# A layer norm and the products around it, made in two halves of the tokens

## The chip, the cores and the metric

The kernel runs on one core of a Trainium2 chip. The metric is the device time of one launch in microseconds. A core has a matrix engine (PE, with its weight loads PEld), a vector engine (DVE), a scalar engine (ACT), a general engine (POOL) and a queue that mostly issues DMAs (SP). Each works through its own list of instructions in order and waits for the others by semaphores.

## The reference, cut to what matters

Two streams of tokens go through a trunk of two layers: x (512 tokens of 1024 features) and ctx (256 tokens), which share all weights. Each layer has three sub-layers, and each ends in a layer norm over the features of a token:

```
def post_norm(x, h, g, b):
    return layer_norm(DEEPNORM_ALPHA * x + h, g, b)
def modulate(h, m, i):
    return h * (1.0 + m[:, :, 3 * i + 1]) + m[:, :, 3 * i]
def swiglu(u, wg, wu, wd):
    return (jax.nn.silu(u @ wg) * (u @ wu)) @ wd
def half_ffn(h, m, i, wg, wu, wd, g, b):
    u = modulate(h, m, i)
    return post_norm(h, 0.5 * m[:, :, 3 * i + 2] * swiglu(u, wg, wu, wd), g, b)
...
h_x = half_ffn(h_x, m_x, 0, ...)                                   # 1024 -> 2816 -> 1024
mix_x, mix_c = token_mixing(modulate(h_x, m_x, 1), modulate(h_c, m_c, 1), ...)
h_x = post_norm(h_x, m_x[:, :, 5] * (mix_x @ w_out[l]), ...)
h_x = half_ffn(h_x, m_x, 2, ...)
```

`token_mixing` is one input projection followed by gated linear attention, windowed attention and an RWKV recurrence. The ctx stream needs no output of its last mixing, so only x runs to the end. So x passes six layer norms, and each lies between a product that makes its input (the FFN's second product with `wd`, or `w_out`) and a product that needs its output (the FFN's first products with `wg` and `wu`, or the input projection); the sixth makes the output.

## The kernel before, in words

Everything is kept feature-major: a tile is 128 features by all tokens of the stream, and a stream (`X`, 512 columns, or `C`, 256) has KT = 8 such tiles. Every product is made in a split float32: weights and data are cut into hi + lo, and each k-tile takes three matmuls, hi x hi, hi x lo and lo x hi (`product`, line 348 the matmul). A weight block of up to four k-tiles is loaded by `load_split`: a DMA, an ACT copy that rounds to hi (line 323), and a subtraction for lo (line 326), alternately on DVE and POOL. Two matmul operands can be seen in a row's name: `pyx<-hhx,l_dx` is the bank `py` of x, from the hidden tile's hi part and the lo part of the weight block `d`.

An FFN makes 22 hidden tiles (`hidden(m)`: banks `pg` and `pu`, then `sg`, `hh`, `hl`), in six groups of four or three. After each group it makes eight tiles `py` of the second product and adds each to the residual `r[j]` on DVE (line 437). In the last group `ln_stat` runs beside it: the sum of r over the feature tiles in `acc1` (POOL, line 470) and that of the squares in `acc2` (ACT squares, line 467; DVE adds, line 472). `wout` does the same with the eight tiles `po` of the output projection.

Then `ln_next` makes the norm. `ln_apply` sums over partitions on PE (banks `lnst`, `lnsq`, line 488), makes mean and 1 / deviation of the 512 tokens (`lnms`: DVE, ACT and a DVE reciprocal, line 505), spreads both over all partitions on PE (`lnm`, `lnb`, line 493) and subtracts the mean from the eight r tiles (line 515: three on DVE, five on POOL). Then for each tile: `ut` on DVE (line 538), its hi part `uh` on ACT (line 543), its lo part `ul` on DVE (line 544; for two tiles of eight on POOL, line 354). The next product starts with `uh0`. The residual of the next sub-layer, alpha * h, is made after the last `ul`: eight instructions on DVE (line 548) and eight on ACT. At the end `ln_out` writes the output (line 558 on DVE, then ACT, then a DMA) in place of u.

The order of the work is fixed when the program is built: the code is written as a sequence, and a scheduler of the build lays out each engine's list from it by its own estimates of what will be ready first. Two streams' stages written one after the other may thus run beside each other: the first stages of x run beside the mixing of ctx, and from about 2020 us on x is alone (its second layer's mixing runs from about 2690 to 3075 us, its last part to the end).

The six norms of x stand in the trace of before at about 881 us (after the first FFN; its next product is the input projection), 1848 (after `wout` of layer 0), 2273 (between the two FFNs), 2654 (before the second input projection), 3123 (after `wout` of layer 1) and 3502 us (the end). They are called the first to the sixth norm below. The ctx stream's first norm, at 285 us, runs with 256 columns.

## Time and profile before

| | us |
|---|---|
| time, median of 3 runs | 3524.95 (3523.06 to 3531.83) |
| span of the profiled execution, first to last instruction | 3523.2 |
| PE busy | 3295.0 (94%) |
| DVE, POOL, ACT busy | 1824.8 (52%), 1513.6 (43%), 1489.5 (42%) |
| x alone, before the third norm (2100 to 2200): PE busy | 100% |
| around the third norm (2200 to 2300): PE busy, granted clock | 87.3%, 0.90 |
| around the fourth (2600 to 2700) | 81.1%, 0.88 |
| around the fifth (3100 to 3200) | 90.7%, 0.93 |

The profiled execution's span is its own time within what the three runs scatter; nothing of size lies around it. [...] PE is full between the norms and has a gap at each of them, and a table by stretches of time shows how long each engine worked in a gap.

### The profile page before, as it was taken

The page shows a single profiled execution, that of the slowest core. Times are in us where ns is not written, and L with a number is a line of the kernel's source. Part 1 is how long each engine was busy: PE and PEld are TensorE (multiplying, and loading weights), DVE is VectorE, ACT ScalarE, POOL GpSimd, SP SyncE. Part 2 cuts the span into 40 slices and gives each one's busy share as a digit, 9 for nine tenths or more (in the row PEclk, how much of TensorE's full clock was granted, in tenths as well). Part 3 has the DMA queues.
Part 4 walks back from the last instruction along what each step waited for, and adds up shares of the span by engine and source line. Part 5 has one row for each costly group of instructions (what it writes and reads, how often), then busy time and mean ns, then how long its engine had stood idle before and what let it go on. Part 6 is the DMA issues. An engine that isn't in the chain of part 4 may idle for free. (4 is left out here: it accounts for less than half of the span.)

```text
span 3523.2 us, 63899 instructions
## 1 busy us (share of the span) xinstructions
PE 3295.0 (94%) x24774; PEld 2668.2 (76%) x24774; DVE 1824.8 (52%) x3198; ACT 1489.5 (42%) x2835; POOL 1513.6 (43%) x1375
## 2 busy tenths in 40 slices
PE   7999999999899999999989999899997997889997
PEld 4797667776677788789867888688885765678886
DVE  2545453445865556566767332542237666762224
ACT  2445333444553445456644433343335335643233
POOL 2554432434644455564454333533345343263335
PEclk8999999999999999999999999999998987999999
DMA  8765444344355543334242333223322210033332
GB/s 300 238 193 172 138 123 136 127 128 142 125 160 181 175 123 115 101 101 130 92 126 65 103 100 96 82 88 98 96 87 72 62 49 11 30 102 96 96 96 75
DMA packets 279135, 407.77 MB, mean 116 GB/s; under 512 B 76464, under 2 KB 101040, under 8 KB 278832
## 3 DMA queue, kind: packets, MB, share of 16 engines
q1 hardware_dynamic: 272064, 397.53, 36.2%
q10 hardware_dynamic: 6768, 6.16, 0.6%
q8 instruction: 195, 3.19, 0.4%
q14 instruction: 108, 0.88, 0.1%
HBM read 390.20 MB, written 13.39 MB: 115 GB/s over the span
## 5 line engine op out<-in xcount | busy, mean ns | idle before, releaser
L348 PE MATMUL pyx<-hhx,l_dx 128*128 128x512 f32 x704 | 277.7, 395 | 4.4 <-DVE l_dx L326 3.2
L348 PE MATMUL pyx<-hhx,h_dx 128*128 128x512 f32 x704 | 275.5, 393 | 0.3 <-ACT h_dx L323 0.3
L348 PE MATMUL pyx<-hlx,h_dx 128*128 128x512 f32 x704 | 275.5, 391 | 0.0
L437 DVE SCALAR_TENSOR_TENSOR rx<-pyx,gtx,rx 128x512 f32<-128x512 f32 x192 | 143.0, 748 | 239.2 <-PE pyx L348 239.1
L326 POOL TENSOR_TENSOR l_ux<-r_ux,h_ux 128x512 fp32r<-128x512 f32 x88 | 114.5, 1301 | 316.5 <-ACT h_ux L323 308.8
L323 ACT ACTIVATE h_dx<-r_dx 128x512 fp32r<-128x512 f32 (+1 forms) x192 | 113.5, 595 | 297.3 <-PE pyx L348 117.8
L323 ACT ACTIVATE h_ux<-r_ux 128x512 fp32r<-128x512 f32 x176 | 111.0, 631 | 280.0 <-PE pgx L348 137.7
L348 PE MATMUL pgx<-uhx,h_gx 128*128 128x512 f32 x528 | 209.2, 396 | 16.1 <-ACT uhx L543 16.1
L323 ACT ACTIVATE h_gx<-r_gx 128x512 fp32r<-128x512 f32 x176 | 111.0, 630 | 267.1 <-PE pyx L348 93.7
L348 PE MATMUL pgx<-ulx,h_gx 128*128 128x512 f32 x528 | 207.6, 393 | 5.9 <-DVE ulx L544 5.9
L326 POOL TENSOR_TENSOR l_dx<-r_dx,h_dx 128x512 fp32r<-128x512 f32 (+1 forms) x96 | 117.4, 1225 | 215.0 <-ACT h_dx L323 201.3
L326 POOL TENSOR_TENSOR l_gx<-r_gx,h_gx 128x512 fp32r<-128x512 f32 x88 | 120.0, 1363 | 204.4 <-ACT h_gx L323 196.0
L348 PE MATMUL pgx<-uhx,l_gx 128*128 128x512 f32 x528 | 207.4, 393 | 0.0
L348 PE MATMUL pux<-uhx,h_ux 128*128 128x512 f32 x528 | 207.1, 392 | 0.0
L348 PE MATMUL pux<-uhx,l_ux 128*128 128x512 f32 x528 | 206.5, 391 | 0.0
L348 PE MATMUL pux<-ulx,h_ux 128*128 128x512 f32 x528 | 206.4, 391 | 0.0
L354 POOL TENSOR_TENSOR hlx<-sgx,hhx 128x512 fp32r<-128x512 f32 x88 | 115.2, 1309 | 151.7 <-ACT hhx L353 151.4
L326 DVE TENSOR_TENSOR l_ux<-r_ux,h_ux 128x512 fp32r<-128x512 f32 x88 | 64.4, 731 | 205.9 <-ACT h_ux L323 205.3
L277 PE MATMUL ada<-wa,sc 128*32 128x256 f32 x1152 | 147.5, 405 | 19.7 <-DMA wa<-in_ada 14.2
L348 PE MATMUL pyc<-hhc,h_dc 128*128 128x256 f32 x528 | 154.9, 295 | 7.2 <-DVE rc L437 5.6
L348 PEld LDWEIGHTS pyx<-hhx,l_dx 128*128 128x128 f32 x704 | 132.6, 188 | 37.3 <-DVE l_dx L326 5.2
L348 PEld LDWEIGHTS pyx<-hhx,h_dx 128*128 128x128 f32 x704 | 132.6, 188 | 32.0 <-ACT h_dx L323 3.0
(800 smaller groups left out, 10153.3 us busy)
## 6 DMA issues: line engine op xcount, KB each, us to landing
wa<-in_ada SPq DMA_DIRECT2D x288, 256.0 KB, 3.8
r_gx<-in_wg SPq DMA_DIRECT2D x176, 256.0 KB, 2.7
r_ux<-in_wu SPq DMA_DIRECT2D x176, 256.0 KB, 2.7
r_gc<-in_wg SPq DMA_DIRECT2D x132, 256.0 KB, 3.0
r_uc<-in_wu SPq DMA_DIRECT2D x132, 256.0 KB, 3.0
r_dx<-in_wd SPq DMA_DIRECT2D x128, 256.0 KB, 2.7
r_dc<-in_wd SPq DMA_DIRECT2D x96, 256.0 KB, 3.0
r_ix<-in_win SPq DMA_DIRECT2D x84, 256.0 KB, 2.7
```

Of the source, the lines that this page charges most:

```text
L277: nc.tensor.matmul(ps[32 * g:32 * g + 32, :256], self.sc[:, k, 6 - 2 * cc:38 - 2 * cc], w[:, x, :], start=cc == 0 and k < 4, stop=cc == 3 ...
L323: nc.scalar.activation(hi[:, :n], raw[:, :n], AF.Copy)
L326: e.tensor_tensor(lo[:, :n], raw[:, :n], hi[:, :n].bitcast(F32), ALU.subtract)
L348: nc.tensor.matmul(ps[:, :N], wt[:, k, :], mv[kk][:, :N], start=kk == 0 and a == 0, stop=kk == n - 1 and a == 2)
L354: self.nc.gpsimd.tensor_tensor(lo, src, hi.bitcast(F32), ALU.subtract)
L437: nc.vector.scalar_tensor_tensor(r[j], py[:, :n], gt[:, j:j + 1], r[j], ALU.mult, ALU.add)
```

## The change

The columns of x are cut into two halves of 256 tokens (`Stream.halves`); ctx has one. Four things are then done by halves:

- The last group of an FFN and the output projection are made in two passes over the eight feature tiles (`passes`), the first for half 0, the second for half 1. Each product has 256 columns instead of 512. The second pass begins with those feature tiles whose split weights are still held (`keep`; four tiles of eight in the FFNs of `rest`, two in `wout`, one in the first FFN); the weights of the others are loaded and split again.
- After each pass `after(h)` makes the norm of that half: sums, reciprocal, spread, subtraction, u and alpha * h. The instructions are as many as before for each half, with half the columns.
- The first hidden tile of the FFN behind a norm, and the first tile of the input projection (number 6), are made half by half, with their weights kept between.
- The scratch tiles `uf`, `sq`, `ut` and `lnms` share one pool of six buffers of 256 columns; sums and mean share one PSUM bank.

Besides, the spreading of the statistics takes a broadcast column (`eq`) in place of a loaded matrix (`eg`), the banks `pg` and `pu` of a hidden tile are claimed together, and the mixing's outputs change places (RWKV to tiles 2 and 3, attention to 4 to 7, the rows of `w_out` with them). Comments are removed, so line numbers shift: the matmul stays line 348, the split of weights becomes 319 and 322, the residual 452, the sums 484, 491 and 495, the statistics 512 to 530, the subtraction 540, u 576 to 582, alpha * h 587, the output 603.

```diff
...
+        self.halves = [slice(c, c + 256) for c in range(0, n, 256)]
...
-    def product(self, ps, ap, mh, ml, n, N, name, lane="f"):
         nc = self.nc
         step = self.step(n)
         for k0 in range(0, n, step):
             w = min(step, n - k0)
-            hi, lo = self.pre.pop((name, k0), None) or self.load_split(ap, k0, w, f"{name}_{k0}", lane)
+            key = name, k0
+            wt2 = self.kept.pop(key, None) or self.pre.pop(key, None)
+            hi, lo = wt2 or self.load_split(ap, k0, w, f"{name}_{k0}", lane)
+            if keep:
+                self.kept[key] = hi, lo
             for k in range(w):
                 for a, (wt, mv) in enumerate(((hi, mh), (hi, ml), (lo, mh))):
                     kk = k0 + k
-                    nc.tensor.matmul(ps[:, :N], wt[:, k, :], mv[kk][:, :N],
+                    nc.tensor.matmul(ps[:, cols], wt[:, k, :], mv[kk][:, cols],
                                      start=kk == 0 and a == 0, stop=kk == n - 1 and a == 2)
+    def passes(self, s, units):
+        nk = (self.wpool["f"][2] - 1) // units if len(s.halves) > 1 else 0
+        order = list(range(KT))
+        for h, cols in enumerate(s.halves):
+            for pos, j in enumerate(order):
+                yield h, cols, pos, j, h == 0 and j >= KT - nk
+            order = list(range(KT - nk, KT)) + list(range(KT - nk - 1, -1, -1))
...
-            pg = pmm("pg" + nm)
-            self.product(pg, self.ins["wg"][f, l, m], s.uh, s.ul, KT, n, "g" + nm)
-            pu = pmm("pu" + nm)
-            self.product(pu, self.ins["wu"][f, l, m], s.uh, s.ul, KT, n, "u" + nm)
+            pg, pu = pmm("pg" + nm), pmm("pu" + nm)
+            parts = s.halves if m == 0 and normed else [slice(0, n)]
+            for cols in parts:
+                keep = cols is not parts[-1]
+                self.product(pg, self.ins["wg"][f, l, m], s.uh, s.ul, KT, cols, "g" + nm, keep=keep)
+                self.product(pu, self.ins["wu"][f, l, m], s.uh, s.ul, KT, cols, "u" + nm, keep=keep)
...
-            for j in range(KT):
-                py = pmm(f"py{s.name}{l}{f}_{gi}_{j}")
-                self.product(py, self.ins["wd"][f, l, j, :, k0:k1], hh, hl, k1 - k0, n, f"d{s.name}{l}{f}_{gi}_{j}")
-                nc.vector.scalar_tensor_tensor(r[j], py[:, :n], gt[:, j:j + 1], r[j], ALU.mult, ALU.add)
+            for h, cols, pos, j, keep in (self.passes(s, 1) if k1 == FT else
+                                          ((0, slice(0, n), j, j, False) for j in range(KT))):
+                py = pmm(f"py{s.name}{l}{f}_{gi}_{j}_{h}")
+                self.product(py, self.ins["wd"][f, l, j, :, k0:k1], hh, hl, k1 - k0, cols, f"d{s.name}{l}{f}_{gi}_{j}",
+                             keep=keep)
+                nc.vector.scalar_tensor_tensor(r[j][:, cols], py[:, cols], gt[:, j:j + 1], r[j][:, cols],
+                    self.ln_stat(s, h, pos, j, r, pool)
+                    if pos == KT - 1:
+                        after(h)
...
+        if pos < KT - 2:
+            nc.gpsimd.tensor_tensor(s.acc1[:, cols], s.acc1[:, cols], r[j][:, cols], ALU.add)
+        else:
+            s.last.append(r[j][:, cols])
+        if pos < KT - 1:
...
+        q = 64
+        ps = self.pln("lnst")
+        sv = ps[:, 0:q], ps[:, q:2 * q]
...
+                nc.tensor.matmul(ps[:, g * q:(g + 1) * q], self.c["eq"][:, g:g + 1].to_broadcast([P, P]), t,
+                                 start=True, stop=True)
+        stat(0, s.acc1[:, cols], True, False)
+        stat(0, s.last[0], False, False)
+        stat(0, s.last[1], False, True)
+        stat(1, s.acc2[:, cols], True, False)
...
+        mean, rs = s.shift[:, cols], s.acc2[:, cols]
+        mb = ps[:, 256:512]
         spread(mb, ms[:, 0])
-        nc.scalar.activation(mean, mb[:, :n], AF.Copy)
-        b = self.pln("lnb")
+        nc.scalar.activation(mean, mb, AF.Copy)
+        b = self.pmm("lnb")[:, 0:256]
         spread(b, ms[:, 2])
-        nc.scalar.activation(rs, b[:, :n], AF.Copy)
+        nc.scalar.activation(rs, b, AF.Copy)
         for j in range(KT):
             e = nc.gpsimd if j >= 3 else nc.vector
-            e.tensor_tensor(r[j], r[j], mean, ALU.subtract)
+            e.tensor_tensor(r[j][:, cols], r[j][:, cols], mean, ALU.subtract)
         return rs
...
+        def after(h):
+            cols = s.halves[h]
+            if h == 0:
+                vectors()
+            if h == len(s.halves) - 1:
+                prefetch()
+            A, B, ag = v["A"], v["B"], v["ag"]
+            rs = self.ln_apply(s, h, r, pool)
             for j in range(KT):
-                nc.vector.scalar_tensor_tensor(r[j], r[j], ag[:, 0, j:j + 1], rs, ALU.mult, ALU.mult)
-                nc.scalar.activation(r[j], r[j], AF.Identity, bias=ag[:, 1, j:j + 1])
-                if rdst is not None:
-                    nc.sync.dma_start(rdst[:, j, :], r[j])
+                hi, lo, rj = s.uh[j][:, cols], s.ul[j][:, cols], r[j][:, cols]
+                t = pool.tile([P, 256], F32, name="ut", tag="uf", bufs=UF)
+                nc.vector.scalar_tensor_tensor(t, rj, A[:, j:j + 1], rs, ALU.mult, ALU.mult)
+                if j in (2, 5):
+                    nc.scalar.activation(t, t, AF.Identity, bias=B[:, j:j + 1])
+                    self.split(hi, lo, t)
+                else:
+                    nc.scalar.activation(hi, t, AF.Identity, bias=B[:, j:j + 1])
+                    last = nc.vector.scalar_tensor_tensor(lo, t, B[:, j:j + 1], hi.bitcast(F32), ALU.add, ALU.subtract)
+            with self.tc.issue_after(last.ins):
+                for j in range(KT):
+                    rj = r[j][:, cols]
+                    nc.vector.scalar_tensor_tensor(rj, rj, ag[:, 0, j:j + 1], rs, ALU.mult, ALU.mult)
+                    nc.scalar.activation(rj, rj, AF.Identity, bias=ag[:, 1, j:j + 1])
+                    if rdst is not None:
+                        nc.sync.dma_start(rdst[:, j, cols], rj)
...
+        for h, cols, pos, j, keep in self.passes(s, 2):
+            py = self.pmm(f"po{s.name}{l}_{j}_{h}")
+            self.product(py, self.ins["wout"][l, j], s.mh, s.ml, KT, cols, f"o{s.name}{l}_{j}", keep=keep)
+            nc.vector.scalar_tensor_tensor(r[j][:, cols], py[:, cols], gt[:, j:j + 1], r[j][:, cols], ALU.mult, ALU.add)
+            self.ln_stat(s, h, pos, j, r, pool)
+            if pos == KT - 1:
+                after(h)
...
```

The order of the instructions on two engines around the third norm follows. Names are tile, head or layer and group numbers: `pyx01_5_7` is the FFN product of x in layer 0, FFN 1, group 5 (the last), feature tile 7, and after the change a last `_0` or `_1` tells the half. On PE before, from the last product of the pass to the first product behind the norm:

```order
L348 MATMUL pyx01_5_7_25292<-hhx01_21_25140,l_dx01_5_7_0_25296 128x512
L488 MATMUL lnst_25360<-acc1_25161,c_ones_m_132 32x128 [waits Pool_49]
L488 MATMUL lnst_25360<-rx1_6_22061,c_ones_m_132 32x128 [waits DVE_49]
L488 MATMUL lnsq_25361<-acc2_25162,c_ones_m_132 32x128 [waits DVE_49]
L488 MATMUL lnst_25360<-rx1_7_22062,c_ones_m_132 32x128 [waits DVE_49]
L488 MATMUL lnsq_25361<-sq_25309,c_ones_m_132 32x128 [waits Activation_49]
L493 MATMUL lnm_25388<-lnms_25382,c_eg_22053 128x128 [waits DVE_49]
L493 MATMUL lnb_25394<-lnms_25382,c_eg_22053 128x128 [waits DVE_49]
L348 MATMUL pgx10_0_25458<-uhx0_1_0_25320,h_gx10_0_0_25338 128x512 [waits Activation_49]
```

And on PE after, from the last product of half 0 to the first of half 1:

```order
L348 MATMUL pyx01_5_7_0_26051<-hhx01_21_25899,l_dx01_5_7_0_26055 128x256
L512 MATMUL lnst_26095<-acc1_25920,c_ones_m_132 32x64 [waits PE_49,Pool_49]
L512 MATMUL lnst_26095<-rx1_6_22365,c_ones_m_132 32x64 [waits DVE_49]
L512 MATMUL lnst_26095<-rx1_7_22366,c_ones_m_132 32x64 [waits DVE_49]
L512 MATMUL lnst_26095<-acc2_25921,c_ones_m_132 32x64 [waits DVE_49]
L512 MATMUL lnst_26095<-sq_26068,c_ones_m_132 32x64 [waits Activation_49]
L517 MATMUL lnst_26095<-lnms_26116,c_eq_142 128x64 [waits DVE_49]
L517 MATMUL lnb_26127<-lnms_26116,c_eq_142 128x64 [waits DVE_49]
L348 MATMUL pyx01_5_4_1_26191<-hhx01_19_25582,h_dx01_5_4_0_25990 128x256
```

What moved: half of the pass's products now stand behind the statistics of half 0, and the same block of statistics comes a second time behind them (not shown). PE goes through its list in order, so the products of half 1 are not issued until the statistics of half 0 have been made. On DVE before, behind the reciprocal of the same norm:

```order
L505 RECIPROCAL lnms_25382<-lnms_25382 128x128 [waits Activation_49]
...
L544 SCALAR_TENSOR_TENSOR ulx6_1_0_25334<-ut_25434,Bx1_0_25312,uhx6_1_0_25326 128x512 [waits Activation_49]
L544 SCALAR_TENSOR_TENSOR ulx7_1_0_25335<-ut_25438,Bx1_0_25312,uhx7_1_0_25327 128x512 [waits Activation_49]
L548 SCALAR_TENSOR_TENSOR rx1_0_22055<-rx1_0_22055,agx1_0_25317,acc2_25162 128x512
...
L548 SCALAR_TENSOR_TENSOR rx1_7_22062<-rx1_7_22062,agx1_0_25317,acc2_25162 128x512
L326 TENSOR_TENSOR l_ux10_1_0_25557<-r_ux10_1_0_25554,h_ux10_1_0_25556 128x512 [waits DMAHW6_49,PE_49,Activation_49]
```

And on DVE after, behind the reciprocal of half 0, with the work of both halves in one list:

```order
L530 RECIPROCAL lnms_26116<-lnms_26116 128x64 [waits Activation_49]
...
L582 SCALAR_TENSOR_TENSOR ulx1_1_0_26088<-ut_26145,Bx1_0_26071,uhx1_1_0_26080 128x256 [waits Activation_49]
L452 SCALAR_TENSOR_TENSOR rx1_4_22363<-pyx01_5_4_1_26191,gtx0_2_23714,rx1_4_22363 128x256 [waits PE_49]
L322 TENSOR_TENSOR l_dx01_5_2_0_26274<-r_dx01_5_2_0_26271,h_dx01_5_2_0_26273 128x384 [waits DMAHW1_49,Activation_49]
...
L582 SCALAR_TENSOR_TENSOR ulx7_1_0_26094<-ut_26171,Bx1_0_26071,uhx7_1_0_26086 128x256 [waits Activation_49]
L587 SCALAR_TENSOR_TENSOR rx1_0_22359<-rx1_0_22359,agx1_0_26076,acc2_25921 128x256
...
L587 SCALAR_TENSOR_TENSOR rx1_7_22366<-rx1_7_22366,agx1_0_26076,acc2_25921 128x256
L495 TENSOR_TENSOR acc2_25921<-acc2_25921,sq_26215 128x256 [waits Activation_49]
L452 SCALAR_TENSOR_TENSOR rx1_3_22362<-pyx01_5_3_1_26249,gtx0_2_23714,rx1_3_22362 128x256 [waits PE_49]
L322 TENSOR_TENSOR l_gx10_0_4_26339<-r_gx10_0_4_26336,h_gx10_0_4_26338 128x512 [waits DMAHW5_49,Activation_49]
...
L526 COPY lnms_26375<-lnst_26354 128x64 [waits PE_49]
L530 RECIPROCAL lnms_26375<-lnms_26375 128x64 [waits Activation_49]
```

What moved: u of half 0 and the residuals, squares and weight splits of half 1 (lines 452, 495, 322) share DVE's list, and alpha * h of half 0 (line 587) now stands ahead of most of half 1's sums and thus ahead of the second reciprocal.

## Rows read from the trace of the kernel before

**Rows 1.** Stretches: length, each engine's busy us (instructions), granted clock, DMA share, GB/s.

```profile
2100.00:2200.00 100.00, 100.00 (x443) 82.81 (x442) 29.29 (x44) 29.38 (x48) 30.39 (x24) 1.00 0.31 96
2200.00:2300.00 100.00, 87.31 (x395) 69.47 (x394) 56.81 (x71) 37.38 (x65) 54.77 (x39) 0.90 0.24 74
```

**Rows 2.** Stretches at the third norm: pass, statistics, making u, rest of hidden tile.

```profile
2253.60:2270.20 16.60, 16.60 (x72) 13.17 (x71) 12.23 (x14) 8.00 (x14) 11.40 (x8) 1.00 0.31 96
2270.20:2282.60 12.40, 6.83 (x58) 4.25 (x56) 10.40 (x15) 5.50 (x11) 5.68 (x5) 0.72 0.23 78
2282.60:2298.60 16.00, 8.89 (x23) 6.55 (x24) 15.87 (x17) 6.64 (x10) 9.58 (x6) 0.57 0.00 0
2298.60:2303.70 5.10, 5.10 (x24) 4.22 (x23) 5.10 (x8) 3.75 (x6) 1.78 (x1) 1.00 0.00 0
```

**Rows 3.** DVE's timeline, third norm: start, us, instruction, idle before and its releaser.

```profile
2259.03 1.41 DVE L437 SCALAR_TENSOR_TENSOR rx<-pyx,gtx,rx 128x512 f32<-128x512 f32 x2 [4.05 <-PE pyx L348]
```

**Rows 4.** Waits, third norm: who waited for whom, us in total, times, longest.

```profile
PE pgx L348 <- ACT uhx L543: 5.8, 1, 5.8
```

**Rows 5.** DVE's groups by form, 2100 to 2310: count, busy us, mean ns, idle before.

```profile
L437 DVE SCALAR_TENSOR_TENSOR rx<-pyx,gtx,rx 128x512 f32<-128x512 f32 x31 | 23.1, 748 | 37.9 <-PE pyx L348 37.9
L538 DVE SCALAR_TENSOR_TENSOR ut<-rx,Ax,acc 128x512 f32<-128x512 f32 x8 | 8.6, 1119 | 0.0
L472 DVE TENSOR_TENSOR acc<-acc,sq 128x512 f32<-128x512 f32 x6 | 8.6, 1426 | 0.2
L548 DVE SCALAR_TENSOR_TENSOR rx<-rx,agx,acc 128x512 f32<-128x512 f32 x8 | 6.4, 870 | 0.0
L544 DVE SCALAR_TENSOR_TENSOR ulx<-ut,Bx,uhx 128x512 fp32r<-128x512 f32 x6 | 6.0, 1046 | 0.1
L326 DVE TENSOR_TENSOR l_dx<-r_dx,h_dx 128x384 fp32r<-128x384 f32 x8 | 4.5, 558 | 9.3 <-ACT h_dx L323 9.3
L515 DVE TENSOR_TENSOR rx<-rx,shift 128x512 f32<-128x512 f32 x3 | 4.0, 1397 | 0.8 <-ACT shift L509 0.8
```

**Rows 6.** DVE's groups by form, 160 to 305, ctx's 256 columns.

```profile
L437 DVE SCALAR_TENSOR_TENSOR rc<-pyc,gtc,rc 128x256 f32<-128x256 f32 x32 | 15.2, 480 | 16.9 <-PE pyc L348 16.8
L538 DVE SCALAR_TENSOR_TENSOR ut<-rc,Ac,acc 128x256 f32<-128x256 f32 x8 | 5.5, 740 | 0.6 <-ACT acc L512 0.6
L472 DVE TENSOR_TENSOR acc<-acc,sq 128x256 f32<-128x256 f32 x6 | 4.1, 692 | 1.3 <-ACT sqt L476 1.2
L544 DVE SCALAR_TENSOR_TENSOR ulc<-ut,Bc,uhc 128x256 fp32r<-128x256 f32 x6 | 3.4, 603 | 0.1
L548 DVE SCALAR_TENSOR_TENSOR rc<-rc,agc,acc 128x256 f32<-128x256 f32 x6 | 2.5, 476 | 0.0
L515 DVE TENSOR_TENSOR rc<-rc,shift 128x256 f32<-128x256 f32 x3 | 2.3, 801 | 0.0
```

**Rows 7.** Stretches at ctx's first norm: pass, statistics, making u.

```profile
273.90:285.30 11.40, 9.89 (x74) 8.93 (x72) 9.26 (x16) 6.32 (x14) 8.28 (x9) 1.00 0.01 2
285.30:290.20 4.90, 3.44 (x54) 2.33 (x53) 2.71 (x8) 3.23 (x9) 0.56 (x1) 1.00 0.61 191
290.20:302.80 12.60, 12.60 (x73) 9.68 (x72) 11.50 (x20) 6.50 (x16) 8.33 (x9) 1.00 0.66 218
```

**Rows 8.** A stretch of PE within ctx's FFN, all matmuls with 256 columns.

```profile
210.00:220.00 10.00, 10.00 (x86) 1.00 0.67 197
```

**Rows 9.** Stretches at the fifth norm: pass, rest of the hidden tile.

```profile
3076.90:3123.00 46.10, 46.10 (x195) 37.62 (x196) 24.06 (x23) 15.86 (x28) 33.61 (x23) 0.94 0.48 154
3145.20:3150.20 5.00, 5.00 (x24) 4.14 (x23) 5.00 (x8) 4.32 (x8) 1.67 (x1) 1.00 0.00 0
```

**Rows 10.** Stretches at the sixth norm: pass, statistics, output.

```profile
3483.00:3499.50 16.50, 16.50 (x73) 13.33 (x71) 9.72 (x14) 5.58 (x11) 8.71 (x7) 1.00 0.05 12
3499.50:3506.60 7.10, 3.96 (x49) 2.98 (x48) 5.50 (x8) 4.24 (x8) 2.64 (x2) 0.76 0.00 0
3506.60:3519.30 12.70, 1.16 (x8) 0.97 (x8) 12.36 (x11) 5.63 (x10) 8.45 (x5) 0.73 0.25 95
```

More of the change, by code (lines that the diff above doesn't have):

```diff
@@ L29 @@
 GMAX = 5
+UF = 6
 NMOD = 9
@@ L212, in setup @@
         self.nsplit = 0
-        self.nada, self.tail, self.pre = 8, None, {}
+        self.nada, self.tail, self.pre, self.kept = 8, None, {}, {}
         self.wnames = []
```

181 lines of the change are left out of this document (79 added, 102 removed).

## The prediction

> **What bounds the kernel now.** I read the table of stretches first. Where x is alone and no norm is near, PE is busy for all of 100 us and does 443 matmuls of 512 columns, 226 ns each, while DVE works 29 us [rows 1]. The stretch with the third norm has the same work in it and PE is busy 87.3 us; DVE's share doubles [rows 1]. So the time is PE's, except at the six norms, and there I asked which engine PE waits for.
>
> The table of the third norm, cut at its steps, answers that [rows 2]. The reader should see three things. In the pass (2253.6 to 2270.2) PE does 72 matmuls without a gap. While u is made (2282.6 to 2298.6) DVE is busy 15.87 of 16.0 us and PE gets 23 matmuls done, at a granted clock of 0.57. The waits name the releaser as ACT's `uh`, 5.8 us for the first one [rows 4], but ACT is busy 6.64 of the 16.0 us [rows 2] and only rounds what DVE has made. So the gap is as long as DVE's list: from the first product to the last u it takes 45.0 us, of which DVE is busy 12.23 + 10.40 + 15.87 = 38.5 and idle 6.5, most of that the 4.05 us ahead of the first residual [rows 2, 3]. The first hidden tile ends 5.1 us later, at +50.1 us from the pass's first product.
>
> **The change part by part.** *Matmuls.* 864 matmuls of 512 columns become twice as many of 256. In ctx's FFN 86 of these take 10.0 us [rows 8], 116 ns each, so a pair costs 232 instead of 226: some 5 us in all if every one were on the path. At the FFN norms they are not, since DVE sets the time there; at `w_out` they are in the sums below.
>
> *DVE's list at an FFN norm.* Per norm it has eight residuals, six additions of squares, three subtractions, eight `ut`, six `ul`, eight alpha * h. With 512 columns that is 8 x 0.748 + 8.6 + 4.0 + 8.6 + 6.0 + 6.4 = 39.6 us [rows 5]. How long they take with 256 columns beside x's POOL work, no trace shows; ctx's first norm has the same instructions with 256 columns: 8 x 0.480 + 4.1 + 2.3 + 5.5 + 3.4 + 8 x 0.476 = 23.0 us [rows 6], 0.58 of it, so two halves take 45.9. What counts is what lies before the last u. Before: 39.6 less alpha * h, 33.2. After: 45.9 less alpha * h of half 1 alone (3.8), and the four reloaded weight blocks, two of them split on DVE at 0.558 [rows 5]: 43.2. So DVE has 10.0 us more to do. The other end is that a half costs exactly a half: 39.6 - 3.2 + 1.1 = 37.5, 4.3 us more, of which alpha * h of half 0, now ahead of half 1's sums, is three quarters.
>
> *Idle time of DVE there.* PE's list has the statistics of half 0 ahead of all products of half 1, so nothing of half 1 fills them. The first residual comes earlier, since its product has half the columns (about -2.0 us of the 4.05). The statistics now stop DVE twice; ctx's took 4.9 us with DVE busy 2.71 [rows 7], so +2.2. Idle: 6.5 - 2.0 + 2.2 = 6.7.
>
> *What is gained.* Products of half 1 run beside u of half 0, and hidden half 0 beside u of half 1. Behind the last u only the second product of hidden half 1 is left, 24 x 0.116 = 2.8 us instead of 5.1.
>
> *Third norm.* Last u at 38.5 + 10.0 + 6.7 = 55.2 (49.5 with exact halves), hidden tile done at 58.0 (52.3) against 50.1: +2.2 to +7.9. I take **+6**, nearer to ctx's rows, which are the same instructions beside the same subtractions on POOL, but a little less, since x's first modulation ran beside them.
>
> [...]
>
> *Fourth norm* (towards the input projection). The same list; but before, the next weights were split behind 6.4 us of alpha * h, and now behind 3.8, so the range falls by 2.5: 0 to +5.5, taken **+4**.
>
> *Sixth norm* (the output). DVE is busy 9.72 + 5.50 + 12.36 = 27.6 of 36.3 us and idle 8.7 [rows 10]. Its list is residual, squares, subtraction and output, the last taken as `ut`: 27.2 us with 512 columns, 2 x 15.7 = 31.5 in halves, and 1.1 of reloads: +5.4; idle as above +0.2. The other end: exact halves (+1.1), and idle time down to 4.5, because the sums on POOL, which DVE waits for there, also halve. Range -3 to +6, taken **+4**.
>
> *Fifth norm* (`w_out`, then the FFN). Here PE is busy throughout the pass, 46.1 us, and DVE only 24.06 of it [rows 9], so room exists. Before, from first product to the end of the hidden tile: 73.3 us (3076.9 to 3150.2). After: half 0's pass 192 x 0.116 = 22.3; statistics, during which PE is idle, 4.9 [rows 7]; the pass of half 1, 22.3 by PE, but DVE then owes u (11.2), alpha * h (3.8), residuals and squares (7.9) and about eight splits (twelve reloaded blocks and four of the FFN, half of them on DVE, at 0.558 x 4/3): 28.8; statistics 4.9; u 9.3 to 11.2; tail 2.8. That is 66.5 to 74.9, so -6.8 to +1.6; taken **-2**. The *second norm* is the same beside ctx's recurrence, where DVE has more to do: -5 to +5, taken **0**. The *first* (first FFN, then the input projection): one feature tile's weights are kept instead of four, so seven are split again; and ctx's `w_out` products, which filled x's gap, stand behind the second statistics in PE's list now. The trace has no pair to price this; between the fourth norm's gain undone and its worst: -2 to +9, taken **+3**.
>
> The loaded matrix that goes, the banks claimed together and the exchanged outputs I cost at nothing: the DMA ends long before its use, and the output products wait for all eight mixing tiles at either order but for a few matmuls.
>
> **Sum.** 6 + 4 + 4 - 2 + 0 + 3 = +15 us on the profiled 3523.2, 3538; the median of the runs is 1.75 above that span, so **3540 us**. Lows add up to -15, highs to +35.
>
> **Rivals.**
> 1. *The gap closes*: PE set free at +16.3 (11.4 + 4.9, rows 7) does half 1's products in 8.4, then statistics 4.9, u at exact half cost 9.3, tail 2.8: +41.7 instead of 50.1, -8.4. With the fourth alike, the fifth and second at -6.8, the first at -5 and the sixth at 0: -36, **3489**. [...] For it speaks the second half of the gap, in which PE does a third of its pace. Against it: DVE would have to do u and alpha * h of half 0 and residuals and squares of half 1, 22 us or more, in the 8.4 us of PE's pass, and it was saturated already (15.87 of 16.0, rows 2).
> 2. *It cancels*: `w_out` norms at their low ends pay for the FFN norms: within 10 us, **3525**. For it: halves that cost a half put the sum near -5. Against: alpha * h of half 0 is in the window at any price.
> [...]
> 4. That the halves don't overlap at all: in PE's list half 1's products stand behind the statistics of half 0, but ahead of anything that needs u, so this is excluded.
>
> **How the numbers follow.** What a measurement of this kernel can tell from no change is about 0.3%, 10.6 us. My forecast (norms longer, above 3535.5) 0.39, rival 3 0.12: slower 0.51. Rival 2: 0.22. Rival 1 and the stretch between it and no change, with the low ends of all terms: 0.27. The forecast's own range is 3528 to 3556; to hold 8 in 10 it must take in rival 2, most of rival 3 and the upper part of rival 1's side: 3503 to 3568.
>
> **What would show it.** At the third norm of the changed kernel: DVE busy almost without a gap from the first residual to the last u, last u at about 55 us from the pass's first product; PE idle through the statistics of half 0 and waiting on residuals (its banks) in the second pass; 256-column instructions at 0.58 of the 512-column ones. At the fifth: a second pass of some 25 us. I am wrong if the second pass runs at PE's pace (8.4 us) with the sums of half 1 done right behind it, if DVE's instructions take half or less, or if the `w_out` norms give more than 7 us each.

## The result, and the profile after

The changed kernel takes 3620.49 us (median; 3610.66 to 3628.0) against 3524.73: 1.027 of it, 95% interval 1.0249 to 1.0288. It is slower, as forecast, but by 95.8 us where 15 were forecast, far above the range. Its profiled execution spans 3618.6 us; PE's busy time grows from 3295.0 to 3357.2 us, DVE's from 1824.8 to 1880.7, and the mean granted clock (TensorE's, as a share of full speed) falls from 0.959 to 0.947.

Where the time went is read by cutting both traces at the first residual addition on DVE of the last group of each FFN, and of the first group of the next. A residual of 256 columns comes about 2 us earlier than one of 512 (the first at the third norm 3.5 us behind the start of its pass, before 5.4), so an FFN is taken together with the norm behind it; while ctx runs beside x, ctx's residuals make the cuts. In us, of one profiled execution each; behind the column of before, differences from it (e3, e4, e12 and e15 are experiments, below):

| stretch | before | forecast | after | e3: no halves | e15: u in halves | e4: norm in halves | e12: whole `w_out`, alpha * h last |
|---|---|---|---|---|---|---|---|
| start, to x's first residual | 403.6 | none | +12.8 | -3.4 | -3.8 | +12.5 | +13.6 |
| x's first FFN and first norm | 644.7 | +3 | +9.7 | -4.4 | -1.0 | +10.0 | +12.5 |
| ctx's FFNs, first mixing, second norm | 891.2 | 0 | +21.4 | -7.1 | -1.8 | +22.3 | -4.1 |
| FFN and third norm | 411.3 | +6 | +8.4 | -0.4 | -0.7 | +4.7 | +15.0 |
| FFN, fourth norm, second mixing | 738.6 | +4 | +8.4 | +2.6 | +9.3 | +12.1 | +10.1 |
| fifth norm (`w_out`) | 107.8 | -2 | +26.3 | -2.6 | -2.7 | +6.2 | +5.1 |
| FFN and sixth norm | 325.8 | +4 | +8.5 | +0.4 | -0.3 | +4.2 | +8.2 |

The first three rows, where ctx runs beside x, move easily: an edit that takes nothing but one matrix out of the kernel before (e16, below) has -1.9, -5.8 and +5.7 there. The largest item is the fifth norm, for which a gain was forecast. The pieces of the third norm answer to [rows 2]: pass and statistics of half 0, u of half 0 beside the pass of half 1, statistics and u of half 1. Columns: length, busy us (instructions) of PE, its weight loads, DVE, ACT, POOL, then granted clock, DMA share, GB/s.

```profile
2293.00:2305.50 12.50, 11.34 (x82) 10.38 (x80) 7.96 (x16) 6.07 (x13) 7.39 (x8) 1.00 0.34 101
2305.50:2310.50 5.00, 2.45 (x46) 2.22 (x46) 2.60 (x7) 1.81 (x6) 1.49 (x2) 0.65 0.04 12
2310.50:2335.00 24.50, 16.61 (x92) 15.46 (x95) 23.11 (x41) 15.32 (x36) 15.71 (x16) 0.71 0.22 66
2335.00:2341.00 6.00, 3.05 (x48) 2.57 (x44) 3.45 (x8) 0.90 (x4) 1.24 (x1) 0.50 0.26 83
2341.00:2353.00 12.00, 12.00 (x76) 12.00 (x76) 11.11 (x20) 5.73 (x14) 6.07 (x7) 0.71 0.01 1
```

DVE is busy 23.11 of the 24.5 us of the middle piece: it is the engine that half 1's products wait for. Its groups there (2295 to 2356) answer to [rows 5]; columns as there.

```profile
L576 DVE SCALAR_TENSOR_TENSOR ut<-rx,Ax,acc 128x256 f32<-128x256 f32 x16 | 11.3, 759 | 0.0
L587 DVE SCALAR_TENSOR_TENSOR rx<-rx,agx,acc 128x256 f32<-128x256 f32 x16 | 8.0, 570 | 0.0
L452 DVE SCALAR_TENSOR_TENSOR rx<-pyx,gtx,rx 128x256 f32<-128x256 f32 x16 | 7.3, 474 | 2.8 <-PE pyx L348 2.7
L582 DVE SCALAR_TENSOR_TENSOR ulx<-ut,Bx,uhx 128x256 fp32r<-128x256 f32 x12 | 7.0, 606 | 0.2 <-ACT uhx L581 0.2
L495 DVE TENSOR_TENSOR acc<-acc,sq 128x256 f32<-128x256 f32 x12 | 6.2, 517 | 0.6 <-ACT sqt L499 0.2
L540 DVE TENSOR_TENSOR rx<-rx,shift 128x256 f32<-128x256 f32 x6 | 4.3, 774 | 3.0 <-ACT shift L534 3.0
```

The six groups together take 44.1 us; the forecast had 45.9. The waits of PE there (2293 to 2345: whom it waited for, us in total, times, longest) show it waiting in the pass of half 1 for the residuals that free its banks and, three times, for the sums:

```profile
PE pyx L348 <- DVE rx L452: 7.3, 4, 4.0
PE lnst L512 <- POOL acc L491: 2.9, 2, 2.4
PE lnst L512 <- DVE acc L495: 2.0, 1, 2.0
```

The fifth norm in the same columns, against [rows 9]: pass of half 0 (three pieces), pass of half 1, and the time until its statistics can begin (two pieces).

```profile
3140.00:3150.00 10.00, 8.61 (x50) 8.09 (x51) 1.57 (x2) 3.79 (x7) 6.92 (x5) 0.67 0.80 266
3150.00:3162.00 12.00, 4.81 (x33) 3.99 (x33) 8.87 (x9) 4.59 (x9) 12.00 (x10) 0.93 0.47 158
3162.00:3178.00 16.00, 16.00 (x115) 15.87 (x115) 8.00 (x11) 5.56 (x11) 10.64 (x10) 0.84 0.43 142
...
3182.00:3205.50 23.50, 23.50 (x196) 23.27 (x194) 16.18 (x24) 9.65 (x18) 16.45 (x16) 1.00 0.38 124
3205.50:3212.30 6.80, 0.50 (x19) 0.27 (x17) 5.91 (x9) 5.41 (x14) 4.30 (x4) 0.69 0.45 148
3212.30:3219.40 7.10, 0.44 (x8) 0.20 (x8) 6.67 (x17) 5.13 (x13) 0.00 (x0) 0.50 0.13 44
```

The second pass goes at PE's own pace, but the first takes 38.0 us for its 192 matmuls (3139.8 to 3177.8), and behind the second PE stands idle for 14 us. Two views say why. The first is that of the waits; PE's, from 3140 to 3250:

```profile
PE pox L348 <- ACT h_ox L319: 8.6, 4, 3.2
PE lnst L512 <- DVE acc L495: 6.7, 1, 6.7
PE lnst L512 <- DVE rx L1636: 6.5, 2, 6.3
```

Of the 8.6 us for `h_ox`, 2.5 lie before the pass's first matmul. Within the pass PE waits 6.0 us for `h_ox` and 2.6 for `l_ox`, which is 8.6 again, and is busy for 29.4 us instead of 22.3, at a mean granted clock of 0.82. DMA from 3138 to 3178 moved 185 GB/s; its issues (count, KB each, median us to landing) are the weights and the residual tiles:

```profile
r_ox<-in_wout SPq DMA_DIRECT2D x18, 256.0 KB, 2.9
rx<-spillx SPq DMA_DIRECT2D x8, 256.0 KB, 5.1
```

and ACT, which rounds the weights, waited in that time:

```profile
ACT h_ox L319 <- DMA r_ox<-in_wout: 9.6, 8, 3.7
ACT h_ox L319 <- PE pox L348: 7.7, 4, 4.6
```

Memory is not all of it. From 3145 to 3150 338 GB/s came in, but from 3155 to 3160, where PE had 1.8 us of work, only 105. POOL is busy for all of the piece from 3150 to 3162: the eight shifts of the residual tiles stand in its list ahead of the lo parts of the next weights (first line, POOL's timeline). The queue of the DMAs waited longer for lo parts, which free the buffers that the weights land in, than for earlier loads (6.8 us):

```profile
3148.84 11.50 POOL L474 TENSOR_TENSOR rx<-rx,shift 128x512 f32<-128x512 f32 x8 [2.34 <-ACT shift L473]
SPq L316 <- DVE l_ox L322: 13.2, 7, 3.5
SPq L316 <- POOL l_ox L322: 6.3, 4, 2.1
```

The kernel before has the same eight shifts, under products that take twice as long for each weight block (226 ns a matmul for 116 [rows 1, 8]). The second view is DVE's timeline behind the second pass (start, us, instructions; in brackets idle time before and its releaser):

```profile
3205.10 0.47 DVE L1636 SCALAR_TENSOR_TENSOR rx<-pox,gtx,rx 128x256 f32<-128x256 f32 x1
3206.46 2.06 DVE L582 SCALAR_TENSOR_TENSOR ulx<-ut,Bx,uhx 128x256 fp32r<-128x256 f32 x2 [0.89 <-ACT uhx L581]
3208.45 1.39 DVE L576 SCALAR_TENSOR_TENSOR ut<-rx,Ax,acc 128x256 f32<-128x256 f32 x2
...
3211.77 0.47 DVE L1636 SCALAR_TENSOR_TENSOR rx<-pox,gtx,rx 128x256 f32<-128x256 f32 x1
...
3213.69 3.24 DVE L587 SCALAR_TENSOR_TENSOR rx<-rx,agx,acc 128x256 f32<-128x256 f32 x8
3216.85 2.53 DVE L495 TENSOR_TENSOR acc<-acc,sq 128x256 f32<-128x256 f32 x5
3220.16 0.23 DVE L526 COPY lnms<-lnst 128x64 f32<-128x64 f32 x1 [0.78 <-PE lnst L512]
```

All products are done at 3205.6, but the last residual and the last sums, on which the statistics wait, stand in DVE's list behind u and, the sums, behind alpha * h of half 0. The sixth norm shows the price of a set of statistics by itself (DVE's timeline; first two lines before, where the subtraction began 3.3 us after the last square was added, then the first set of after):

```profile
3501.68 1.89 DVE L472 TENSOR_TENSOR acc<-acc,sq 128x512 f32<-128x512 f32 x2
3506.88 4.03 DVE L515 TENSOR_TENSOR rx<-rx,shift 128x512 f32<-128x512 f32 x3 [0.33 <-ACT shift L509]
...
3584.29 0.89 DVE L495 TENSOR_TENSOR acc<-acc,sq 128x256 f32<-128x256 f32 x2 [1.06 <-ACT sqt L499]
3585.95 0.23 DVE L526 COPY lnms<-lnst 128x64 f32<-128x64 f32 x1 [0.78 <-PE lnst L512]
3586.53 0.23 DVE L528 TENSOR_TENSOR lnms<-lnst,lnms 128x64 f32<-128x64 f32 x1 [0.35 <-ACT lnms L527]
3587.17 0.55 DVE L530 RECIPROCAL lnms<-lnms 128x64 f32<-128x64 f32 x1 [0.41 <-ACT lnms L529]
3589.23 2.16 DVE L540 TENSOR_TENSOR rx<-rx,shift 128x256 f32<-128x256 f32 x3 [1.51 <-ACT shift L534]
```

The same five steps come again at 3603.74 with the same gaps: each set of 256 columns takes 4.1 us from the last sum to the subtraction, of which DVE is idle 3.05; the granted clock is 0.50 in both.

### The profile page after: what moved, and what is told of

The parts are those of the page before. It is cut to its first block, busy times and chain, and to the rows that moved or that the text cites. A ratio compares the mean times of both kernels' runs of the same rounds, so it can differ in the third digit from the quotient of the medians.

```text
span 3618.6 us, 67207 instructions
## 1 busy us (share of the span) xinstructions
PE 3357.2 (93%) x25980; PEld 2770.8 (77%) x25980; DVE 1880.7 (52%) x3472; ACT 1544.5 (43%) x3062; POOL 1541.5 (43%) x1474
## 5 line engine op out<-in xcount | busy, mean ns | idle before, releaser
L348 PE MATMUL pyx<-hhx,h_dx 128*128 128x512 f32 (+1 forms) x800 | 299.5, 376 | 16.9 <-DVE rx L452 16.0
L348 PE MATMUL pyx<-hhx,l_dx 128*128 128x512 f32 (+1 forms) x800 | 298.8, 375 | 4.8 <-DVE l_dx L322 2.5
L348 PE MATMUL pyx<-hlx,h_dx 128*128 128x512 f32 (+1 forms) x800 | 296.6, 371 | 0.7 <-POOL hlx L364 0.7
L348 PE MATMUL pgx<-uhx,h_gx 128*128 128x512 f32 (+1 forms) x552 | 212.7, 385 | 0.0
L348 PE MATMUL pgx<-uhx,l_gx 128*128 128x512 f32 (+1 forms) x552 | 212.3, 385 | 0.0
L348 PE MATMUL pgx<-ulx,h_gx 128*128 128x512 f32 (+1 forms) x552 | 212.1, 384 | 0.0
L348 PE MATMUL pux<-uhx,l_ux 128*128 128x512 f32 (+1 forms) x552 | 210.5, 381 | 0.0
L348 PE MATMUL pux<-ulx,h_ux 128*128 128x512 f32 (+1 forms) x552 | 210.1, 381 | 0.0
L348 PE MATMUL pux<-uhx,h_ux 128*128 128x512 f32 (+1 forms) x552 | 209.9, 380 | 0.0
L348 PEld LDWEIGHTS pyx<-hhx,h_dx 128*128 128x128 f32 x800 | 155.5, 195 | 48.1 <-ACT rx L588 10.8
L348 PEld LDWEIGHTS pyx<-hlx,h_dx 128*128 128x128 f32 x800 | 156.3, 195 | 24.7 <-POOL hlx L364 1.1
```

Of the source, the lines that this page charges most:

```text
L348: nc.tensor.matmul(ps[:, cols], wt[:, k, :], mv[kk][:, cols], start=kk == 0 and a == 0, stop=kk == n - 1 and a == 2)
```

## The experiments

Ratios are to the kernel before, on the same chip, with 95% intervals. Letters in the quoted texts name theories; what each result decides is said behind it in words.

**Which part costs it: e1, e2, e12.** e1 makes each `w_out` product whole again; norm and the rest stay in halves.

```diff
-        for h, cols, pos, j, keep in self.passes(s, 2):
+        for j in range(KT):
             py = self.pmm(...)
-            self.product(py, ..., cols, ..., keep=keep)
+            self.product(py, ..., slice(0, s.n), ...)
+            for h, cols in enumerate(s.halves):  # residual, ln_stat of each half
...
```

> The changed kernel with the output projection's products whole again (512 columns, one pass); the norm behind it, u and the first hidden tile stay in halves, made one after the other. Theory A (the passes of 256 columns ask for each weight block in half the time, and that starves PE in the first pass at w_out): the stretch from the first residual of w_out in layer 1 to the first residual of the next FFN falls from 134 to about 112 us (108 before), the same at layer 0, together about 40 us less than the changed kernel, near 3580. Theory B (DVE's list around the norm is what is long, whatever the products' width): the stretch stays above 125 us and the time above 3605.

3594.9 us, 1.0196 (1.0181 to 1.0211): 25.6 us come back, by the traces 16.0 at the fifth norm and 9.6 in the stretch of the second. The waits for `h_ox` at the fifth fall from 8.6 to 3.8 us, and within the pass, without the one ahead of its first matmul, from 6.0 to 1.3. e2 makes alpha * h of half 0 only after u of half 1.

```diff
+            if h < len(s.halves) - 1:
+                return
             with self.tc.issue_after(last.ins):
-                for j in range(KT):
+                for cols in s.halves:
+                    for j in range(KT):
...
```

> The changed kernel with alpha * h of half 0 issued behind the last u of half 1. Theory B1 (alpha * h of half 0 stands in DVE's list ahead of the second half's sums, and PE waits for these): 3.2 to 4.7 us less at each of the five norms that make u, so 15 to 22 us less, 3598 to 3605. Rival (something else in the list fills the place, or the sums are late for the split weights and the residuals): within 5 us of the changed kernel, 3615 to 3625.

3608.2, 1.0241 (1.0212 to 1.0269): 12 us come back, which is little against the scatter of both (the intervals of the two ratios overlap); by the traces 8.8 in the stretch of the second norm, some 4 at the third and in the row of the fourth, 2 at the fifth. So alpha * h is in the way as forecast. e12 has both edits:

> The changed kernel with both the products of w_out whole (e1) and alpha * h of half 0 last (e2). If the two costs are separate, the gains of e1 (25 us) and e2 (12 us) add: 3578 to 3588. If alpha * h only mattered behind the passes of w_out, no more than e1: 3592 to 3598.

3584.65, 1.0163 (1.0136 to 1.0189). The two add up; 60 us of the 96 are elsewhere. The table's last column shows where: at the fifth norm 21 of the 26 us are gone, and in the row of the second norm all 21 and 4 more, though both norms are still made in halves with two sets of statistics (the row behind it takes 6.7 back).

**Halves or the rest of the change: e3, e4, e7.** e3 makes one part of 512 columns. With it the scratch tiles go back to two buffers of 512 columns, and sums and mean to banks of their own (left out below); all else of the change is kept.

```diff
-        self.halves = [slice(c, c + 256) for c in range(0, n, 256)]
+        self.halves = [slice(0, n)]
...
```

> The changed kernel with one half of all 512 columns, so only the rest of the change is left (broadcast column, banks pg and pu claimed together, exchanged mixing outputs, the norm written as a function that is called at the end of the pass). Theory C (halves alone cost the time): 3520 to 3532, as the kernel before. Rival D (the rest of the change moved the scheduler's order, which the stretches of ctx and of x's first FFN, 6 to 8 us longer each, suggest): 3540 or more.

3515.1, 0.9967 (0.9954 to 0.998). So the rest of the change gains about 10 us, which the sum had at nothing, and the halves, with their shared scratch buffers, cost 105. e4 makes all products whole, and norm, first tiles and first modulation in halves:

> The changed kernel with both kinds of products ahead of a norm whole (last FFN group and output projection), only the norm, u and the first tiles behind it in halves, one half after the other. If the halves of the norm by themselves cost DVE 0.58 of the whole each (Theory B), each of the six norms is 4 to 6 us longer than before: 3550 to 3560. If the passes are what costs (Theory A, at the FFNs too), it comes near the kernel before, 3520 to 3535.

3598.3, 1.0201 (1.0185 to 1.0218). To take the passes away gives back only 22 of the 105: most is lost with no pass at all. e7 is e3 with the first tiles behind a norm in halves:

> e3 with only the first hidden tile of an FFN behind a norm and the first tile of the input projection made in halves. All of u is needed for the second half, but PE may no longer take the next tile's products between them: before, three banks took turns while u came in. Theory F (this turn-taking is lost): 3 to 5 us at each of five norms, 3530 to 3540. Rival: only 144 + 24 pairs of matmuls at 6 ns, 3515 to 3518.

3521.65, 0.9998 (0.9986 to 1.0011): 6.6 us over e3, between the two. By the traces it lies in the rows of the second norm (7.5) and the first (3.1), beside ctx; the third and fourth are as in e3, so theory F's loss at each norm is not seen.

**Norm, passes and modulation alone: e5, e6, e8, spoiled.** Each adds one part to e3, but also scratch tiles under a new tag, of 4 KB a partition: e5 the first modulation in halves, e6 the norm in halves, e8 the two passes with the norm whole.

> e3 (no halves) with x's and ctx's first modulation alone in halves of 256 columns. Theory E (x's 8 first modulations become 16 smaller sets on DVE, ACT and POOL and slow ctx's first FFN beside them, which is why the stretches up to x's first residual are 12 to 16 us longer in every kernel with halves): 3525 to 3531. Rival (these stretches are longer because the scheduler's order changed for another reason): 3512 to 3518.

> e3 with only the norm (statistics, u, alpha * h) in two halves, made one after the other behind whole products; the products behind it and the first modulation are whole. Theory B (DVE's instructions with 256 columns cost 0.58 of the whole and the statistics are made twice): 5 to 9 us at each of six norms, 3545 to 3570. If a norm in halves costs little by itself: 3515 to 3530.

> e3 with only the products and residuals ahead of a norm in two passes of 256 columns, sums by halves, and the norm, u and everything behind it whole. Theory A (weight blocks are wanted at twice the rate in the first pass at w_out, and reloaded): about 20 us at each w_out, 2 to 4 at an FFN, 3555 to 3575. Rival (passes cost only through what the norm's halves put between them): 3518 to 3528.

3640.6, 3704.8 and 3729.8 us (1.034, 1.0516 and 1.0582): all above what any theory gave, and not for the reason tested. In e5 the first matmul of x's first FFN comes at 496.9 us, in e3 at 284.8. PE between is half empty (first line e5, second e9, which is the same kernel without the new tag; columns as above):

```profile
340.00:480.00 140.00, 77.53 (x918) 63.94 (x918) 61.03 (x126) 38.01 (x88) 32.12 (x44) 0.66 0.11 26
```

```profile
290.00:400.00 110.00, 104.92 (x696) 81.51 (x694) 58.71 (x106) 57.38 (x115) 49.90 (x69) 1.00 0.50 156
```

x's first FFN, which else runs beside ctx's mixing, starts after it. The totals say nothing of the parts. Stretches away from there can be read. e6, the norm in halves behind whole products, has +9.4, +10.8 and +4.2 in the rows of the third, fifth and sixth norms, where e3 has -0.4, -2.6 and +0.4: so the norm in halves costs that by itself. At the fifth norm e8, passes with one set of statistics, needs 125.3 us against 105.2 in e3, and PE there waits for the weights' rounding as in after:

```profile
PE pox L349 <- ACT h_ox L320: 8.5, 4, 2.7
```

POOL there makes the eight shifts in one piece of 11.05 us too. So the slow first pass belongs to the passes and needs no second norm. e9 repeats e5 in the buffers that are there:

```diff
-        for cols in s.halves:
-            uf = pool.tile([P, s.n], F32, name="uf", tag="uf", bufs=2)
+        for cols in [slice(c, c + 256) for c in range(0, s.n, 256)]:
+            uf = pool.tile([P, s.n], F32, name="uf", tag="uf", bufs=2)[:, 0:256]
```

> e3 (no halves) with x's and ctx's first modulation in halves of 256 columns, in the same two scratch buffers as e3, so that no pool grows (in e5 the added scratch kept x's first FFN from starting beside ctx's mixing, 200 us). Theory E (the modulation in halves lengthens the stretches up to x's first residual by some 15 us and the kernel by about 9 to 15): 3524 to 3530. Rival (the modulation costs nothing once memory is the same): 3512 to 3518.

3511.1, 0.9961 (0.9949 to 0.9972): e3's time. The modulation in halves costs nothing by itself, in two buffers, so the theory that it does falls.

**Smaller suspects: e10, e11, e13.** e10 is e3 with the bank `pu` claimed only after `pg`'s product:

> e3 with the bank pu claimed behind pg's product again, as in the kernel before. If the common claim is what made e3 about 10 us faster than the kernel before: 3522 to 3528. If it is another part (the broadcast column in place of a loaded matrix, the order of the mixing outputs): 3512 to 3518.

3511.9, 0.9959 (0.9945 to 0.9974): nothing hangs on the claim. e11 puts the first hidden tile's half 0 ahead of the statistics of half 1 in PE's list, so that these don't hold it up:

```diff
             if h == len(s.halves) - 1:
                 prefetch()
+                if h and i != 1:
+                    self.early = [self.pmm(x + nm) for x in ("pg", "pu")]
+                    ... # both products with s.halves[0], keep=True
```

> The changed kernel with half 0 of the first hidden tile written ahead of the statistics of half 1, so that PE has it to do while DVE finishes half 1's sums. Theory B (DVE's list is the bound and the hidden tile of half 0 is hidden beside u of half 1 anyway): no gain, 3612 to 3628. Rival G (PE's list, in which half 0's hidden products stand behind half 1's statistics, is what costs): 5 us less at each of the three FFN norms, 3600 to 3608.

3610.1, 1.0234 (1.0202 to 1.0267). The norms stay: the third's stretch is 103.8 us after 104.5, the fifth's 134.9 after 134.2. The 10 us come from stretches that the edit doesn't touch, more than half of them from that of the second mixing (-5.6). So the order on PE is not what holds the norm; DVE's list is. e13 is after with three buffers instead of six in the scratch pool of `uf`, `sq`, `ut` and `lnms` (`UF = 3`):

> The changed kernel with three scratch buffers of 256 columns instead of six. Theory H (with six, x's first modulation runs at once and takes DVE from ctx's first FFN; with two, in e9, it was spread out and nothing was lost): the stretches up to x's first residual are 10 to 16 us shorter, and the kernel is at 3603 to 3612 unless the norms, whose u goes through the same buffers, get longer by as much. Rival (these stretches are longer for another reason): no change there, 3615 to 3640 by the norms.

3613.4, 1.0256 (1.0237 to 1.0275). x's first residual comes at 406.2 us instead of 416.4, but by the end of the first norm all of it but 0.5 us is given back: the table's first two rows together are +22.0, in after +22.4. What is left of the 7 us in time lies in stretches of x alone, and the intervals of the two ratios overlap. The stretch 145 to 180 us in after and in e13 shows why x's first residual moves:

```profile
145.00:180.00 35.00, 25.88 (x160) 24.95 (x159) 25.48 (x46) 15.00 (x34) 23.24 (x24) 0.76 0.38 125
```

```profile
145.00:180.00 35.00, 28.21 (x219) 26.15 (x218) 31.65 (x51) 18.23 (x40) 27.71 (x27) 1.00 0.54 176
```

PE does 160 matmuls instead of 219. With six buffers DVE's list has six of x's modulations ahead of a residual of ctx (after, DVE's timeline):

```profile
146.41 3.27 DVE L399 TENSOR_SCALAR uf<-rx,Ax,Bx 128x256 f32<-128x256 f32 x6
150.21 0.47 DVE L452 SCALAR_TENSOR_TENSOR rc<-pyc,gtc,rc 128x256 f32<-128x256 f32 x1
```

**Shorter instructions or a second set of statistics: e15.** e7 with subtraction, `ut` and `ul` in halves, as many instructions as in after, but sums and statistics made once for 512 columns, and alpha * h whole:

```diff
-            for j in range(KT):
+            for cols, j in [(c, j) for c in s.uh2 for j in range(KT)]:
+                if j == 0:
+                    ... # subtract the mean from this half of all eight r
                 t = pool.tile([P, s.n], F32, name="ut", tag="hh", bufs=GMAX)[:, 0:256]
```

> e7 (no halves but the first tiles) with the subtraction, u and its lo part in halves behind statistics made once for all 512 columns. Theory B1 (DVE's instructions with 256 columns cost more than half): 20 instructions more at each of five norms, 3 to 5 us each, 3535 to 3548. Theory B2 (what a norm in halves costs is that its sums and statistics are made twice, one behind the other, in lists that run in order): within 5 us of e7, 3517 to 3527, while e4, with statistics by halves, is at 3598.

3523.9, 1.0008 (0.9995 to 1.0021): 2 us over e7. From the first residual to the last u of the third norm it takes 41.4 us, e4 49.2, e3 39.6 (in this order; columns as above):

```profile
2252.80:2294.20 41.40, 29.50 (x177) 24.29 (x176) 39.26 (x58) 21.69 (x43) 26.13 (x24) 0.79 0.16 51
```

```profile
2300.40:2349.60 49.20, 30.89 (x222) 26.97 (x221) 44.77 (x84) 25.82 (x62) 25.67 (x28) 0.72 0.14 44
```

```profile
2244.40:2284.00 39.60, 27.09 (x130) 19.82 (x130) 37.33 (x40) 18.84 (x32) 25.40 (x16) 0.74 0.17 54
```

After needs 53.5. So shorter instructions for u cost 1.9 us of DVE (39.26 against 37.33), and what e4 adds to e15, residuals, squares, statistics and alpha * h by halves, 5.5 more of DVE and 2.3 of its idle time. Of the 5.5, 3.3 are alpha * h of half 0, which in e15 comes behind the last u. In the whole kernel e4 is 74 us above e15; in this the first modulation in halves and the shared pool of six buffers are contained, so the 74 are not all the second set's.

Nor is a second set always paid in full. At the sixth norm e4 makes the two sets side by side, and both together take 3.7 us from the last square to the subtraction; its row there is +4.2, where after, with the sets one behind the other, has +8.5.

**The gain of e3: e16.** Before, with the broadcast column in place of the loaded matrix alone:

> The kernel before with the broadcast column eq in place of the loaded matrix eg, nothing else. If this is why e3 is about 10 us faster than the kernel before (a load of 256 KB and 2 KB per partition less in each work pool): 3510 to 3518. If it is the mixing outputs' order or the form of the norm: 3521 to 3528.

3520.6, 0.9989 (0.9978 to 0.9999), 0.3 us from the median of the kernel before in the same runs: at most a part. Which other part of the rest gives e3 its 10 us (the mixing's order, or the form of the norm's code) stays open. e3, e9 and e10 beat both kernels, by 0.3 to 0.4%.

## Why the prediction was wrong

The profiled execution is 80 us longer than the forecast's sum. By the table's rows, 28 of them lie at the fifth norm, 21 in the row of the second, 19 in the first two rows and 11 at the third, fourth and sixth norms.

**Direction and mechanism.** That DVE's list bounds an FFN norm, that half 1's sums queue behind u and alpha * h of half 0, and that splitting doesn't shorten it: right, by the third norm's rows, e2 and e11. Rival 1 (the gap closes) is out; of rival 2, halves that cost a half, e15 shows something near it for u alone, but not for the norm (e4, e6).

**Third norm, +6 forecast, +8.4 in the table.** Counted as the forecast did, from the first product to the end of the hidden tile, it is 61.6 us (2295.0 to 2356.6) for 50.1: +11.5, above the forecast's +7.9; the FFN around it gives 3.1 back. The last u comes after 57.05 us (55.2 forecast) by two errors that partly cancel: DVE is busy 46.9 us (48.5 forecast; its six groups take 44.1 for 45.9) and idle 10.2 (6.7). Undersized is the idle time: the two sets of statistics were to add 2.2 us, from ctx's first norm [rows 7]. In after DVE is idle 3.4 and 3.05 us through them, by its timeline, and was 1.8 us in before's one set: +4.7. ctx's set ran at a granted clock of 1.00 and these at 0.52 and 0.50, at which the same steps took longer: at the fifth norm their gaps add up to 3.05 us at 0.50 and to 2.24 at 1.00 (last section). Behind the last u 4.5 us are left, not 2.8: hidden half 0 began only at 2342.7 and took 8.1 us, at a granted clock of 0.68. In the **sixth**, +4 forecast and +8.5 measured, the same term was +0.2, and a second set behind the first costs what its rows show, 4.1 us from sum to subtraction. The **fourth**, +4 forecast, has +8.4 together with its mixing; e15, without a second set, has +9.3 there, so this stretch doesn't tell the norm by itself.

**Fifth norm, -2 forecast, +26.3 measured: the step that failed.** It said "half 0's pass 192 x 0.116 = 22.3", by PE's rate. But this pass calls for all sixteen weight blocks, and the eight residual tiles come from memory meanwhile: 24 transfers of 256 KB in 22.3 us would be 282 GB/s, while in before 46.1 us had 154 GB/s [rows 9]. It moved 185; ACT waited 9.6 us for weights to land and 7.7 us for buffers to come free. The pass took 38.0 us: of the 15.7 lost, 8.6 are PE's waits for weights, and 7.1 that it is busy longer with the same matmuls (29.4 us), at a mean granted clock of 0.82. That the passes cost it, e8 (20 us with the passes alone) and e1 (16 back) show. How it splits between the landing of the weights and POOL's shifts, which hold up their lo parts, is read from the waits and not shown by a run. The second part of that step, DVE's 28.8 us from half 1's pass on, was right as work (16.18 + 5.91 + 6.67 = 28.8 busy in the rows of 3182 to 3219.4) and wrong as time: 37.4 us, since DVE waited for `h_ox` and products within the pass and had its u and alpha * h left over when PE was done. That is another 8.6 us. The two, less 1.1 in the smaller pieces, make up the distance between the forecast's upper bound, 74.9, and the 98.1 measured (3139.8 to 3237.9, the end of the hidden tile). For the **second** norm 0 was forecast; with ctx's FFNs and the mixing ahead of it, from which the traces don't part it cleanly, it has +21.4. Whole `w_out` products give 9.6 of that back (e1), alpha * h of half 0 made last 8.8 (e2), and both together all of it (e12, -4.1, of which the next row takes 6.7 back), with two sets of statistics as before. So here the passes and the place of alpha * h in DVE's list cost it, and the second set by itself no more than the few us by which rows beside ctx move. That e4, with whole products but alpha * h of half 0 in its old place, has +22.3 is more than e1 lets expect; why stays open.

**First norm, +3 forecast, +9.7 measured, and the start, no term and +12.8.** x's first modulation was in the diff and was taken to cost nothing. How the two rows share the +22.4 depends on the number of scratch buffers (e13), their sum hardly. e4 has all of the sum (+22.5) and e9 and e15 none (-5.9 and -4.8). So neither the reloaded weights named in the step nor the modulation in halves by itself makes it, but what e4 has beyond these two runs: residuals, sums, statistics and alpha * h by halves beside ctx's work, with the shared pool. The place of alpha * h in DVE's list is not it (the sum is +23.6 in e2 and +26.0 in e12); which of the others it is, no run parts. Against all this stands -10 for the edits costed at nothing (e3).

**The clock, and rival 3 at 0.12.** The forecast's range took in most of rival 3; no run shows a term for it. In its place the runs show this: the granted clock in the second `w_out` pass was 1.00 (3182 to 3205.5), and it was 0.50 in pieces where PE had been idle before, as in the last piece shown of the fifth norm, where PE is busy for 0.44 of 7.1 us. Where it was low, hidden half 0 of the third norm took 8.1 us for 48 matmuls (at 0.68), where 48 x 0.116 = 5.6, PE was busy for 29.4 us instead of 22.3 in the first pass of `w_out` (0.82), and the statistics had longer waits (last section).

**What a half costs on DVE.** The forecast took 0.58 of the whole. The rows of after against [rows 5] have 0.63 for the residual (474 against 748 ns) and 0.58 for `ul` (606 against 1046), but 0.36 for the squares (517 against 1426). These means mix instructions with and without POOL at work beside them. In before the sums of squares that run while POOL is idle take 411 to 426 ns with 256 columns (six of them) and 675 to 693 with 512 (five), on average 416 and 687, 0.61; the others take 768 and 1249 on average, 0.62. For a norm e15 decides: it pays 1.9 us of DVE at the third for all of u in halves.

## What to carry to other kernels

Before you split a step in two, look at what lies between its input and its output: a chain of small dependent steps, as the statistics of a norm, cost here as much for half the columns (4.1 us from the last sum to the subtraction at the sixth norm, in before 3.3 for all of them), and was paid twice where the two stood one behind the other (that row +8.5; +4.2 in e4, side by side). Where a pass is halved in columns, its weights and whatever else is loaded or made beside it are due in half the time (at the fifth norm 282 GB/s were called for and 185 moved), so price it by the bytes and by the other engines' work for each weight block as well as by matmuls. An engine's amount of work in a stretch is a lower bound of its time there (28.8 us of DVE's work took 37.4 at the fifth norm); read from its list in order what stands ahead of the instruction that the next engine waits for.

## What the hardware showed that was not expected

The second sets of statistics at the third, fifth and sixth norms of after have the same four gaps on DVE, 0.78, 0.35, 0.41 and 1.51 us, and the granted clock is 0.50 in all three, after PE had waited 2.0, 6.7 and 2.5 us for the sums. The first set of the fifth norm, right behind a pass, has 1.00 (3178 to 3182); its gaps are 0.89, 0.29, 0.41 and 0.65 us, the last of them the wait for the spread of the mean on PE. The eight matmuls that spread the mean take 1.10 us there and 1.97 in the second set (PE's timeline):

```profile
3180.27 1.10 PE L517 MATMUL lnst<-lnms,c_eq 128*128 128x64 f32 x8 [0.86 <-DVE lnms L528]
3221.02 1.97 PE L517 MATMUL lnst<-lnms,c_eq 128*128 128x64 f32 x8 [0.92 <-DVE lnms L528]
```

So behind the second pass, where the clock fell while PE waited (0.69 and 0.50 from 3205.5 to 3219.4), the wait for the spread itself was longer, 1.51 us for 0.65. Splitting u costs little: 41.4 us in e15 against 39.6 in e3. And a new scratch tag moved the start of x's first FFN by 212 us (496.9 against 284.8 us in e5 and e3); that the pool's memory keeps it from ctx's mixing is an inference from the edits of e5 and e9, and was not shown by itself.
